# Two weight sums per seven-product block made by accumulating transfers, with two plain blocks per layer instead of three

## The chip, the cores and the metric

The kernel runs as one program on one core of a Trainium2 chip. The metric is device time in microseconds (us), from one launch with the data in the chip's memory to the output there. Engines are named as the profile does: PE multiplies matrices, DVE, ACT and POOL work on tiles in on-chip memory (POOL can't read PE's result banks, and doesn't in this kernel), and SP issues most transfers.

## The reference

Two layers of a decoder trunk over 512 tokens, with 16 learned tokens ahead of them (528 columns in layer 0; in layer 1 only the 512 real ones are carried through the projections behind attention). A layer is: RMSNorm, one input projection, an attention group and a retention group, an output projection with residual, then RMSNorm and a SwiGLU feed-forward part (FFN) with residual. All in float32. What matters here is the FFN and the output projection ahead of it:

```
h = h + einsum('blc,cd->bld', mix, w_out)          # 1024 -> 1024
hn = rmsnorm(h, ffn_norm)
ff = silu(hn @ w_gate) * (hn @ w_up)                # 1024 -> 2816, twice
h = h + ff @ w_down                                 # 2816 -> 1024
```

## The kernel before

**Precision.** Every float32 operand of a product is split into a high part (a cast to fp32r, on ACT) and a low part (the value minus its high part, on DVE or POOL). A product is three matmuls: high by high, high by low of the tokens, low of the weight by high. `convert` makes these parts for a weight tile: one cast per 128x512 half (line 180), then the subtraction (line 183), which is one 128x512 instruction on DVE, or four of 128x128 on POOL where a job has `pool` set.

**Tokens lie along columns**, 128 features to a tile, eight tiles `h[k]`. `scale_split` (lines 308, 309) makes `xh`, `xl`, the parts of the scaled tokens. The reciprocal root of the norm, `R`, is made separately (`rstd`, lines 279 to 289) from column sums of squares and multiplied in behind the products.

**The FFN** has 22 blocks of 128 gate and 128 up columns. The first `PLAIN` = 3 blocks of a layer are plain: `dense_steps` runs eight steps for the gate and eight for the up rows, three matmul pairs of 264 columns each in layer 0, three matmuls of 512 columns in layer 1. The other blocks are a `Unit`, which treats gate and up together as a 2x2 block product (rows gate and up, contraction in two halves of four tiles, `HB` = 4, tokens in two column halves of 264 or 256) and needs seven half-size products instead of eight: 84 matmuls. A unit has a head (weights `w1`, the plain gate tile), a middle (`w2`, and the first half of `w3`) and a tail (the second half of `w3`, and `w4`). `w2`, `w3` and `w4` need sums of the weight quarters (`make2`, `make3`, `make4`): four DVE instructions of 128x512 per unit, before their splits (lines 888 and 889). The tokens need sums too, made once per layer by `x_forms` during the plain blocks (four calls; lines 861 to 866, then a split into `th`, `tl`).

**Order.** The blocks go in `ROUNDS` of 3, 4, 4, 4, 4 and 3 blocks. The down-projection of a round stands between the units of the next one, one job per unit: `head, middle, down job, tail, second half of the down job`. A unit of the first round has no down job yet; it goes `head, middle`, and its tail comes behind the head of the next unit. The up product of a unit ends its tail and starts its closing chain: `done` (lines 974 to 986) adds the banks, scales, applies `silu` on ACT, multiplies by the up rows and splits the result into `ah`, `al`, which the down job of the next round multiplies. For plain blocks the same is done by `g_done` (line 836, then `silu`) and `u_done` (lines 844, 845).

PE's order is the order in which the steps are written. The other engines get theirs from the Tile scheduler, which lists each engine's instructions when the program is built; at run time each engine, and each engine's queue of transfers, takes them strictly in that order and waits at the first that isn't ready. `need` makes the weights of the coming jobs one unit ahead.

**Buffers.** Weight tiles arrive in a ring `raw` of three (512 KB each) and, for the units' up rows, `fraw` of two; the split weights sit in `whi`/`wlo` and `fwhi`/`fwlo`, two each. A load is issued by SP as soon as the last reader of the slot is done. In the plain part the reader that frees a `raw` slot is the subtraction of line 183. The first gate product of a layer is held back: its bank `psd` is read only once `R` is there (line 836, during the second gate product), so the second up product needs this bank again.

Of the kernel before, what the change touches and what calls it, by code (L numbers as in the profile page):

```python
# [20 lines left out]
DEPTH = 2  # L21
# [3 lines left out]
DFF = 2816  # L25
NF = DFF // 128
ROUNDS = ((0, 3), (3, 7), (7, 11), (11, 15), (15, 19), (19, 22))
PLAIN = 3
HB = NK // 2
EPS = 1e-6  # L30
NBLK = SEQ // 128
# [8 lines left out]
def hybrid_kernel(ctx, tc, x_t, w_in, w_fl, w_out, w_gate, w_up, w_down, vecs, b_fg, rope, decay, mask, ident, out_t):  # L40
    nc = tc.nc
# [84 lines left out]
    def vcol(c):  # L126
        return vec[:, c:c + 1]
# [58 lines left out]
    def dense_steps(src, parts, pool=False, banks=False, ahead=(1, 4), own=None, wait=None):  # L186

        j = len(jobs)  # L190
        jobs.append({"src": src, "pool": pool, "own": own})

        def chunk(k0, k, n, xs, cols, ps, done):
            def go():
                convert(j)
                if k == 0:
                    t = [psum_a() for _ in cols] if banks else psum()
                    ps.append(t)
                    ps.append(t if banks else [t[:, b] for b in range(2)])
                size = jobs[j]["w"][0][0]  # L200
                _, hi, lo = jobs[j]["w"][(k0 + k) // size]
                wk = (k0 + k) % size
                xh, xl = xs(k)
                for i, (w, x) in enumerate(((hi, xh), (hi, xl), (lo, xh))):
                    for b, (c0, c1) in enumerate(cols):
                        nc.tensor.matmul(ps[1][b][:, 0:c1 - c0], w[:, wk, :], x[:, c0:c1],  # L206
                                         start=(k == 0 and i == 0), stop=(k == n - 1 and i == 2))
# [54 lines left out]
    def fft(tag, dt=F32R, shape=(128, T), bufs=None):  # L262
        return phase["ffn"].tile(list(shape), dt, name=tag, tag=tag, bufs=bufs)
# [28 lines left out]
    RSC = -1.0 / (2.0 * D)  # L292
# [513 lines left out]
    def out_proj(l, rnd, mix, real):  # L806

        cols = REAL if real else FULL
        xs = lambda k: mix[k]["mix"]
        return sum([dense_steps(w_out[l, rnd, m2], [(4 * s, xs, 4, cols, add_h(2 * m2 + s, real)) for s in range(2)],  # L810
                                rnd == 0 or m2 < 2, rnd == 1 and m2 == 1) for m2 in range(NK // 2)], [])

    def ffn(l, st, real, last):
        QC = REAL if real else FULL
# [7 lines left out]
        def two(t):  # L822
            return t[:, t0:T].rearrange("p (a b) -> p a b", a=2)
# [30 lines left out]
        def x_forms(k):  # L854
            def go():
                if k == 0:
                    st["t"] = [[fft(f"t{p}{i}", shape=(128, 2, 4, w)) for p in "hl"] for i in range(2)]
                s = fft("S", F32, (128, 6, w), 2)
                a, b = ((h[k][:, c0:c1], h[HB + k][:, c0:c1]) for c0, c1 in HC)
                g0, g1 = vcol(V_FFN + l * NK + k), vcol(V_FFN + l * NK + HB + k)  # L860
                nc.scalar.activation(s[:, 0:2], two(h[k]), AF.Copy, scale=g0)
                nc.vector.tensor_sub(s[:, 2], s[:, 1], s[:, 0])
                for i in range(2):
                    nc.vector.scalar_tensor_tensor(s[:, 3 + i], b[1], g1, s[:, 1 + i], ALU.mult, ALU.subtract)
                nc.vector.scalar_tensor_tensor(s[:, 5], a[1], g1, s[:, 4], ALU.mult, ALU.subtract)
# [21 lines left out]
        def splits(hi, lo, src):  # L887
            nc.scalar.copy(hi, src)  # L888
            nc.vector.tensor_sub(lo, src, hi.bitcast(F32))  # L889
# [17 lines left out]
        class Unit:  # L907
# [12 lines left out]
            def load(self):  # L920
                if "a" not in self.t:
                    for n, src, pool, tag, bufs in (("a", w_gate, wp, "raw", 3), ("b", w_up, phase["ffn"], "fraw", 2)):
                        self.t[n] = pool.tile([128, NK, 128], F32, name=tag, tag=tag, bufs=bufs)
                        nc.sync.dma_start(self.t[n], src[l, self.f])


            def make1(self, hi, lo):
# [1 line left out]


            def make2(self, hi, lo):
                a, b = self.t["a"], self.t["b"]
                s = self.t["s"] = fft("S", F32, (128, NK, 128), 2)
                nc.vector.tensor_add(s[:, HB:NK], b[:, 0:HB], b[:, HB:NK])
                nc.vector.tensor_sub(s[:, 0:HB], s[:, HB:NK], a[:, 0:HB])
                splits(hi, lo, s)


            def make3(self, hi, lo):
                a, b = self.t["a"], self.t["b"]  # L940
                nc.vector.tensor_sub(b[:, 0:HB], a[:, 0:HB], b[:, 0:HB])
                splits(hi, lo, b)


            def make4(self, hi, lo):
                a, s = self.t["a"], self.t["s"]
                nc.vector.tensor_sub(a[:, HB:NK], a[:, HB:NK], s[:, 0:HB])
                splits(hi, lo, a[:, HB:NK])

            def bank(self, n):  # L950
# [21 lines left out]
            def done(self):  # L972
                e = self.t["e"]
                sg = tt("sg")
                with tc.high_priority():
                    nc.vector.tensor_add(two(sg), self.t["zy"][:, :, 0:w], e[:, 0:2])
# [72 lines left out]
        for r, (f0, f1) in enumerate(ROUNDS):  # L1049
            for f in range(f0, f1):  # L1050
                if f < PLAIN:
                    steps += dense_steps(w_gate[l, f], [(0, xs, NK, QC, g_done(f) if f else held.append)], banks=f == 1)
                    steps += dense_steps(w_up[l, f], [(0, xs, NK, QC, u_done(f))])
                    continue
                u = Unit(f)
                steps += u.head()
                for v in tails:
                    v.last()
                    steps += v.tail()
                tails = []  # L1060
                u.rest()
                steps += u.middle()
                if fills:
                    p, g0, g1 = fills.pop(0)
                    j = down_job(p, g0, g1)
                    steps += down(j, 0, 2 * p, g0, g1, not real)
                    u.last()
                    steps += u.tail()
                    steps += down(j, 1, 2 * p + 1, g0, g1, False)
                else:  # L1070
                    tails = [u]
            for p, g0, g1 in fills:
# [167 lines left out]
        return steps  # L1240

    gf = const.tile([128, NK], F32, name="gf")
    nc.vector.tensor_scalar_mul(gf, vec[:, V_FIN:V_FIN + NK], RSC)

    def layer(l):
# [177 lines left out]
```

## Time and profile before

| | before |
|---|---|
| median of 3 runs | 1268.92 us (1268.71 to 1269.12) |
| profiled execution, its own time | 1268.51 us |
| its span | 1266.7 us |
| PE busy | 1252.7 us, 99% of the span |
| DVE, ACT, POOL busy | 998.3, 686.9, 265.0 us |
| FFN, layer 0: first gate product starts; first unit starts | 287.7; 322.5 us |
| FFN, layer 1: second gate product starts; first unit starts | 923.0; 945.2 us |

The page is one execution taken by the hardware profiler. A timeline row gives the start in microseconds from the span's start, the duration, the engine, the line, the operation, the output and input tiles and shapes, how many such instructions were merged in the row, and in brackets the idle time of the engine before it with what ended it. Instructions of one engine overlap slightly: the distance between two starts is what the engine can hold, and for matmuls this distance, not the duration, is the cost.

### The profile page before, as it was taken

What the parts mean: (1) busy time and instruction counts of PE and PEld (TensorE: products, weight loads), DVE (VectorE), ACT (ScalarE), POOL (GpSimd) and SP (SyncE); (2) the same over time, 40 slices, a digit from 0 to 9 for tenths busy, and PEclk for the clock granted to TensorE, in tenths of its full rate; (3) what the DMA queues carried; (4) which work ended last, traced back from release to release, by engine and by line L of the source; (5) the groups of instructions that cost most, each with busy time, mean ns of one, the idle gap of its engine ahead of it and who ended that gap; (6) DMA issues with size and microseconds to landing.
All of it is one profiled execution on the core that took longest, in us unless ns stands there. A gap on an engine that the chain in (4) does not pass through costs nothing.

```text
span 1266.7 us, 23601 instructions
## 1 busy us (share of the span) xinstructions
PE 1252.7 (99%) x9263; PEld 1195.0 (94%) x9263; DVE 998.3 (79%) x1853; ACT 686.9 (54%) x1246; POOL 265.0 (21%) x526
## 2 busy tenths in 40 slices
PE   9999999999999999999999999999999999999997
PEld 8999999999999999999999989999789999999996
DVE  7878756879988888887786877567898878888867
ACT  7666545676444444444456665457764444444445
POOL 3455546420000000000025546454100000000000
PEclk9999999999999999999999999999999999999999
DMA  6322222223333333332323132222323333333321
GB/s 218 94 69 87 90 86 76 68 68 117 105 97 100 101 101 101 101 100 84 101 77 117 61 102 83 77 91 67 100 91 124 103 100 101 101 100 101 100 83 68
DMA packets 45680, 120.57 MB, mean 95 GB/s; under 512 B 5360, under 2 KB 12272, under 8 KB 45568
## 3 DMA queue, kind: packets, MB, share of 16 engines
q1 hardware_dynamic: 45136, 118.77, 29.5%
q8 instruction: 73, 1.20, 0.4%
q14 instruction: 39, 0.32, 0.1%
q10 hardware_dynamic: 432, 0.29, 0.1%
HBM read 116.91 MB, written 2.13 MB: 94 GB/s over the span
## 4 chain that ended last, share of the span: by engine, by line
PE 94%; DVE 2%; ACT 2%; DMA 1%; issue 0%; DVEq 0%; ACTq 0%; SPq 0%
PE psd L206 30%; PE psa L900 19%; PE psd L1035 14%; PE psd L900 13%; PE psa L206 5%; PE psa L1035 4%; PE psa L407 2%; PE psa L582 2%; PE psa L497 2%; PE psa L749 1%; PE psa L719 1%; DMA h<-x_t 0%; ACT whi L180 0%; PE psa L279 0%; ACT sq L325 0%
## 5 line engine op out<-in xcount | busy, mean ns | idle before, releaser
L183 POOL TENSOR_TENSOR wlo<-raw,whi 128x128 fp32r<-128x128 f32 x504 | 260.8, 551 | 268.1 <-ACT whi L180 247.4
L206 PE MATMUL psd<-xh,whi 128*128 128x264 f32 (+1 forms) x792 | 195.3, 314 | 0.7 <-ACT whi L180 0.6
L206 PE MATMUL psd<-xl,whi 128*128 128x264 f32 (+1 forms) x792 | 186.1, 302 | 0.6 <-DVE xl L309 0.6
L206 PE MATMUL psd<-xh,wlo 128*128 128x264 f32 (+1 forms) x792 | 186.4, 303 | 0.0
L206 PEld LDWEIGHTS psd<-xh,whi 128*128 128x128 f32 x792 | 127.9, 189 | 6.0 <-ACT whi L180 1.6
L206 PEld LDWEIGHTS psd<-xh,wlo 128*128 128x128 f32 x792 | 126.8, 188 | 6.3 <-DVE wlo L183 0.4
L206 PEld LDWEIGHTS psd<-xl,whi 128*128 128x128 f32 x792 | 127.4, 188 | 5.2 <-DVE xl L309 1.2
L180 ACT CAST whi<-raw 128x512 fp32r<-128x512 f32 (+1 forms) x168 | 98.4, 613 | 49.6 <-PE psd L206 36.5
L888 ACT CAST whi<-raw 128x1024 fp32r<-128x1024 f32 (+2 forms) x62 | 54.9, 885 | 50.9 <-PE psd L900 39.5
L888 ACT CAST fwhi<-raw 128x1024 fp32r<-128x1024 f32 (+2 forms) x62 | 55.6, 897 | 47.0 <-PE psd L900 40.0
L85 POOL MEMSET kl<- 64x528 f32 x2 | 1.1, 534 | 345.4 <-PE psa L900 345.4
L889 DVE TENSOR_TENSOR wlo<-raw,whi 128x1024 fp32r<-128x1024 f32 (+2 forms) x62 | 62.9, 1014 | 12.8 <-ACT whi L888 12.7
L889 DVE TENSOR_TENSOR fwlo<-raw,fwhi 128x1024 fp32r<-128x1024 f32 (+2 forms) x62 | 64.0, 1032 | 10.8 <-ACT fwhi L888 10.6
L900 PE MATMUL psa<-th,whi 128*128 128x264 f32 (+1 forms) x232 | 65.4, 282 | 0.0
L900 PE MATMUL psa<-th,wlo 128*128 128x264 f32 (+1 forms) x232 | 65.4, 282 | 0.0
L900 PE MATMUL psa<-tl,whi 128*128 128x264 f32 (+1 forms) x232 | 65.3, 282 | 0.0
L900 PE MATMUL psa<-th,fwhi 128*128 128x264 f32 (+1 forms) x224 | 63.4, 283 | 0.0
L900 PE MATMUL psa<-tl,fwhi 128*128 128x264 f32 (+1 forms) x224 | 63.3, 283 | 0.0
L900 PE MATMUL psa<-th,fwlo 128*128 128x264 f32 (+1 forms) x224 | 63.2, 282 | 0.0
L517 ACT ACTIVATE pd<-pd,nmax 128x144 f32<-128x144 f32 (+1 forms) x64 | 36.9, 576 | 40.7 <-DVE nmax L504 28.8
L966 ACT COPY e<-psa 128x264 f32<-128x264 f32 (+1 forms) x114 | 42.8, 375 | 28.5 <-PE psa L900 24.2
L888 ACT CAST fwhi<-S 128x1024 fp32r<-128x1024 f32 x20 | 21.0, 1049 | 68.6 <-PE psa L900 66.5
(342 smaller groups left out, 4030.3 us busy)
## 6 DMA issues: line engine op xcount, KB each, us to landing
raw<-w_in SPq DMA_DIRECT2D x54, 512.0 KB, 3.5
raw<-w_gate SPq DMA_DIRECT2D x44, 512.0 KB, 3.9
fraw<-w_up SPq DMA_DIRECT2D x38, 512.0 KB, 3.5
raw<-w_down SPq DMA_DIRECT2D x64, 256.0 KB, 2.7
raw<-w_out SPq DMA_DIRECT2D x16, 512.0 KB, 3.5
raw<-w_down SPq DMA_DIRECT2D x32, 192.0 KB, 2.5
bc<-cdr SPq DMA_DIRECT2D x16, 264.0 KB, 3.5
raw<-w_up SPq DMA_DIRECT2D x6, 512.0 KB, 3.5
```

The source lines that it names most:

```text
L180: pin(nc.scalar.copy(hi, job["raw"][:, c0:c1]), pinned)
L183: pin(sub(lo[:, i:i + wide], job["raw"][:, c0 + i:c0 + i + wide], hi[:, i:i + wide].bitcast(F32)), pinned)
L206: nc.tensor.matmul(ps[1][b][:, 0:c1 - c0], w[:, wk, :], x[:, c0:c1], start=(k == 0 and i == 0), stop=(k == n - 1 and i == 2))
L407: nc.tensor.transpose(ps[:, 128 * j:128 * j + 128], src[:, o:o + 128], idt)
L497: nc.tensor.matmul(sc[0:nq, 0:c1 - c0], st["q"][s][:, q0:q0 + nq], kk[:, c0:c1], start=(i == 0), stop=(i == 1))
L517: nc.scalar.activation(pr, pr, AF.Exp, bias=nmax[0:nq], scale=-1.0, accum_out=rsum)
L582: nc.tensor.matmul(po[:, c0:SEQ], v[:, j, :], pp[:, j, META + c0:T], start=(j == 0 and i == 0), stop=(j == 4 and i == 1))
L888: nc.scalar.copy(hi, src)
L889: nc.vector.tensor_sub(lo, src, hi.bitcast(F32))
L900: nc.tensor.matmul(bank()[:, 0:b.shape[-1]], a[:, o + k, :], b, start=(fresh and k == 0 and i == 0), stop=(k == n - 1 and i == 2), skip_gr ...
L966: nc.scalar.copy(self.t["e"][:, i], self.t["x"][:, 0:w])
L1035: nc.tensor.matmul(v[:, 0:c1 - c0], a[:, s * n + k, :], b[:, c0:c1], start=(k == 0 and i == 0), stop=(k == n - 1 and i == 2))
```

## The change

- `PLAIN` is 2: block 2 of each layer becomes a unit. It is in the first round, so it has no down job between its parts, and its tail stands behind the head of block 3.
- In a unit the sum of the up rows' two halves, and the sum of the gate's low half with the up rows' low half, are no longer made by DVE. A new tile `ws` (two buffers) receives the low half of the up rows by a plain transfer of SP, and the high half by a second transfer, issued by POOL, that adds to what is there. A third, also from POOL, adds the gate's low half onto the low half of `fraw`. `make2` keeps one DVE instruction, `make3` none. Signs differ by this (sums instead of differences), which `x_forms` and the scale in `done` take up with a negated column `ngf`.
- The low parts of the last two tiles of the output projection (`m2` = 2, 3) and of all plain gate and up tiles go to POOL, eight 128x128 instructions a tile instead of two of 128x512 on DVE.
- The scratch for the descriptors of POOL's transfers is set to 4096.

```diff
-PLAIN = 3
+PLAIN = 2
@@ out_proj
-                                rnd == 0 or m2 < 2, rnd == 1 and m2 == 1) for m2 in range(NK // 2)], [])
+                                True, rnd == 1 and m2 == 1) for m2 in range(NK // 2)], [])
@@ x_forms
+                n1 = ngf[:, l * HB + k:l * HB + k + 1]
-                nc.vector.tensor_sub(s[:, 2], s[:, 1], s[:, 0])
-                for i in range(2):
-                    nc.vector.scalar_tensor_tensor(s[:, 3 + i], b[1], g1, s[:, 1 + i], ALU.mult, ALU.subtract)
-                nc.vector.scalar_tensor_tensor(s[:, 5], a[1], g1, s[:, 4], ALU.mult, ALU.subtract)
+                nc.vector.tensor_sub(s[:, 2], s[:, 0], s[:, 1])
+                nc.vector.scalar_tensor_tensor(s[:, 3], b[1], g1, s[:, 1], ALU.mult, ALU.subtract)
+                nc.vector.scalar_tensor_tensor(s[:, 4], b[1], n1, s[:, 2], ALU.mult, ALU.subtract)
+                nc.vector.scalar_tensor_tensor(s[:, 5], a[1], n1, s[:, 4], ALU.mult, ALU.subtract)
@@ Unit.load
+                    s = self.t["s"] = fft("ws", F32, (128, NK, 128), 2)
+                    nc.sync.dma_start(s[:, HB:NK], w_up[l, self.f, :, 0:HB])
+                    nc.gpsimd.dma_start(s[:, HB:NK], w_up[l, self.f, :, HB:NK], accum_op=ALU.add)
+                    nc.gpsimd.dma_start(self.t["b"][:, 0:HB], w_gate[l, self.f, :, 0:HB], accum_op=ALU.add)
@@ make2, make3, make4
-                s = self.t["s"] = fft("S", F32, (128, NK, 128), 2)
-                nc.vector.tensor_add(s[:, HB:NK], b[:, 0:HB], b[:, HB:NK])
-                nc.vector.tensor_sub(s[:, 0:HB], s[:, HB:NK], a[:, 0:HB])
+                nc.vector.tensor_add(s[:, 0:HB], s[:, HB:NK], a[:, 0:HB])
-                nc.vector.tensor_sub(b[:, 0:HB], a[:, 0:HB], b[:, 0:HB])
-                nc.vector.tensor_sub(a[:, HB:NK], a[:, HB:NK], s[:, 0:HB])
+                nc.vector.tensor_add(a[:, HB:NK], a[:, HB:NK], s[:, 0:HB])
@@ done
-                nc.vector.scalar_tensor_tensor(u[:, c], sg[:, c], RSC, st["R"][:, c], ALU.mult, ALU.mult)
+                nc.vector.scalar_tensor_tensor(u[:, c], sg[:, c], -RSC, st["R"][:, c], ALU.mult, ALU.mult)
@@ the steps of a plain block
-                    steps += dense_steps(w_gate[l, f], [(0, xs, NK, QC, g_done(f) if f else held.append)], banks=f == 1)
-                    steps += dense_steps(w_up[l, f], [(0, xs, NK, QC, u_done(f))])
+                    steps += dense_steps(w_gate[l, f], [(0, xs, NK, QC, g_done(f) if f else held.append)], True, banks=f == 1)
+                    steps += dense_steps(w_up[l, f], [(0, xs, NK, QC, u_done(f))], True)
```

How the change moves instructions, at three places. In the lists below a row is one instruction, or several alike with their count, in the order in which the engine takes them; `raw` is a weight tile of the ring, `fraw` that of a unit's up rows, `ws` the new sum tile, `whi`/`wlo` and `fwhi`/`fwlo` the split weights.

POOL, from the output projection of layer 0 to the first units, as changed; in the kernel before there are no transfers here, and the row of x264 is one of x232 that ends with the output projection's `m2` = 1:

```order
L183 TENSOR_TENSOR wlo<-raw,whi 128x128 x264
L929 DMA fraw<-w_gate 128x512
L928 DMA ws<-w_up 128x512
L183 TENSOR_TENSOR wlo<-raw,whi 128x128 x8
L929 DMA fraw<-w_gate 128x512
L928 DMA ws<-w_up 128x512
L183 TENSOR_TENSOR wlo<-raw,whi 128x128 x8
L928 DMA ws<-w_up 128x512
L929 DMA fraw<-w_gate 128x512
```

The 32 new subtractions of the x264 are those of `m2` = 2, `m2` = 3, the first gate tile and the first up tile; the two rows of x8 are the second gate and second up tile. The accumulating transfers of blocks 2 and 3 stand ahead of them.

DVE around the making of `R` in layer 0. Before:

```order
L132 TENSOR_TENSOR tl_4309<-S,th_4308 128x1056
L288 SCALAR_TENSOR_TENSOR nwt<-psa,nwt 128x264 x2
L183 TENSOR_TENSOR wlo<-raw,whi 128x512
L289 SCALAR_TENSOR_TENSOR R<-nwt,R 128x528
L183 TENSOR_TENSOR wlo<-raw,whi 128x512
L836 SCALAR_TENSOR_TENSOR sg<-psd,R 128x528
L844 SCALAR_TENSOR_TENSOR tq<-psd,R 128x528
```

As changed:

```order
L286 TENSOR_TENSOR nwt<-R 128x528
L938 TENSOR_TENSOR ws<-ws,raw 128x512
L288 SCALAR_TENSOR_TENSOR nwt<-psa,nwt 128x264 x2
L132 TENSOR_TENSOR tl_4341<-S,th_4340 128x1056
L289 SCALAR_TENSOR_TENSOR R<-nwt,R 128x528
L890 TENSOR_TENSOR fwlo<-ws,fwhi 128x1024
L836 SCALAR_TENSOR_TENSOR sg<-psd,R 128x528
L844 SCALAR_TENSOR_TENSOR tq<-psd,R 128x528
```

The sum of block 2 (line 938), which reads `ws` behind its accumulating transfer, and the low part made from it (line 890) now stand ahead of the row that frees the bank `psd` (line 836).

ACT at the `silu` of the first gate product, layer 0, as changed:

```order
L180 CAST whi<-raw 128x512 x2
L889 CAST fwhi<-ws 128x1024
L889 CAST fwhi<-raw 128x1024
L396 ACT_TABLE_LOAD
L396 ACTIVATE sg<-sg 128x528
L889 CAST whi<-raw 128x1024
L131 CAST ah_4382<-tq 128x528
```

The casts of block 2's `w2` (from `ws`) and of block 3's gate tile (`fwhi<-raw`) stand ahead of the table load, that of block 2's own gate tile (`whi<-raw`) behind the `silu`. In the kernel before no weight cast of a unit stands in this place: the two plain casts `whi<-raw` and two token rows `S` are followed by the table load at once.

More of the change, by code (lines that the diff above doesn't have):

```diff
@@ L931, in make2 @@
             def make2(self, hi, lo):
-                a, b = self.t["a"], self.t["b"]
-                s = self.t["s"] = fft("S", F32, (128, NK, 128), 2)
-                nc.vector.tensor_add(s[:, HB:NK], b[:, 0:HB], b[:, HB:NK])
-                nc.vector.tensor_sub(s[:, 0:HB], s[:, HB:NK], a[:, 0:HB])
+                a, s = self.t["a"], self.t["s"]
+                nc.vector.tensor_add(s[:, 0:HB], s[:, HB:NK], a[:, 0:HB])
                 splits(hi, lo, s)
             def make3(self, hi, lo):
-                a, b = self.t["a"], self.t["b"]
-                nc.vector.tensor_sub(b[:, 0:HB], a[:, 0:HB], b[:, 0:HB])
-                splits(hi, lo, b)
+                splits(hi, lo, self.t["b"])
             def make4(self, hi, lo):
                 a, s = self.t["a"], self.t["s"]
-                nc.vector.tensor_sub(a[:, HB:NK], a[:, HB:NK], s[:, 0:HB])
+                nc.vector.tensor_add(a[:, HB:NK], a[:, HB:NK], s[:, 0:HB])
                 splits(hi, lo, a[:, HB:NK])
@@ L1242, in hybrid_kernel @@
     gf = const.tile([128, NK], F32, name="gf")
+    ngf = const.tile([128, DEPTH * HB], F32, name="ngf")
+    for i in range(DEPTH):
+        c = V_FFN + i * NK + HB
+        nc.vector.tensor_scalar_mul(ngf[:, i * HB:i * HB + HB], vec[:, c:c + HB], -1.0)
     nc.vector.tensor_scalar_mul(gf, vec[:, V_FIN:V_FIN + NK], RSC)
@@ L1410 @@
     }
-    nc = bacc.Bacc("TRN2", target_bir_lowering=False, num_devices=1)
+    nc = bacc.Bacc("TRN2", target_bir_lowering=False, num_devices=1, dynamic_dma_scratch_size=4096)
     arrays, args = {}, []
```

## The prediction

> **What bounds the kernel now.** I read the page first: span, busy times, the chain that ended last; then the waits of PE.
>
> ```profile
> span 1266.7 us, 23601 instructions
> PE 1252.7 (99%) x9263; PEld 1195.0 (94%) x9263; DVE 998.3 (79%) x1853; ACT 686.9 (54%) x1246; POOL 265.0 (21%) x526
> PE 94%; DVE 2%; ACT 2%; DMA 1%; issue 0%; DVEq 0%; ACTq 0%; SPq 0%
> PE psa L1276 <- DVE wide L61: 1.6, 1, 1.6
> PE psa L497 <- DVE kl L441: 0.9, 1, 0.9
> ```
>
> PE is the bound almost everywhere: 94% of the chain, and its longest single wait is 1.6 us, at the very start. So DVE work taken away is worth nothing by itself; only fewer matmuls are, and every wait that the change puts ahead of PE is lost in full. How near PE stands to waiting is seen where the first gate product hands on its bank:
>
> ```profile
> 299.34 0.40 PE L206 MATMUL psa<-xh,whi 128*128 128x264 f32 x2
> 302.58 0.70 DVE L289 SCALAR_TENSOR_TENSOR R<-nwt,R 128x528 f32<-128x528 f32 x1
> 303.20 0.68 DVE L183 TENSOR_TENSOR wlo<-raw,whi 128x512 fp32r<-128x512 f32 x1
> 303.80 0.70 DVE L836 SCALAR_TENSOR_TENSOR sg<-psd,R 128x528 f32<-128x528 f32 x1
> 305.12 0.40 PE L206 MATMUL psd<-xh,whi 128*128 128x264 f32 x2
> ```
>
> The second gate product starts at 299.34, the second up product takes the bank at 305.12, and DVE freed it at 304.5: a margin of 0.6 us.
>
> **The change: matmuls.**
>
> ```profile
> 388.28 2.92 PE psa L1035 x24
> 928.71 16.67 PE psd L206 x72
> 945.22 0.28 PE L900 MATMUL psa<-xh,whi 128*128 128x256 f32 x1
> 952.31 0.39 PE L1035 MATMUL psd<-ah,fwhi 128*128 128x512 f32 x1
> ```
>
> A matmul of 264 columns costs 2.92/24 = 0.1217 us, of 512 columns 16.67/72 = 0.2315; between 945.22 and 952.31 stand head and middle of a unit, 60 of 256 columns, 0.118 each. Layer 0: 96 become 84, 12 x 0.1217 = 1.46 us less. Layer 1: 48 x 0.2315 = 11.11 become 84 x 0.118 = 9.91, 1.20 less. Saved: 2.7 us. That is all the change can give.
>
> **POOL's low parts.** They start behind the casts of the output projection's third tile, and how long eight take depends on DVE:
>
> ```profile
> 273.87 1.14 ACT L180 CAST whi<-raw 128x512 fp32r<-128x512 f32 x2 [4.10 <-PE psd L206]
> L183 POOL TENSOR_TENSOR wlo<-raw,whi 128x128 fp32r<-128x128 f32 x504 | 260.8, 551 | 268.1 <-ACT whi L180 247.4
> 37.36 3.44 POOL L183 TENSOR_TENSOR wlo<-raw,whi 128x128 fp32r<-128x128 f32 x8 [5.22 <-ACT whi L180]
> 83.05 5.27 POOL L183 TENSOR_TENSOR wlo<-raw,whi 128x128 fp32r<-128x128 f32 x8 [4.63 <-ACT whi L180]
> 35.09 1.41 DVE L441 TENSOR_TENSOR kl<-tq,kh 64x528 fp32r<-64x528 f32 x2
> 85.31 0.96 DVE L441 TENSOR_TENSOR kl<-tq,kh 64x528 fp32r<-64x528 f32 x1
> 283.00:300.00 17.00, 17.00 (x141) 16.86 (x140) 16.93 (x30) 11.20 (x19) 0.00 (x0) 1.00 0.44 156
> ```
>
> With POOL idle the same DVE subtraction takes 0.70 us (two in 1.41), beside POOL 0.96; and eight low parts take 3.44 to 5.27. So the two slow each other. From 283 to 300 DVE is busy throughout (third figure, 16.93 of 17; POOL, the fifth, had nothing). I take 8 x 0.551 = 4.41 for the tiles of `m2` = 2 and 3, and 5.27 for the first gate and up tile: from 274.5 (first half cast), 8.8 + 10.5 us, so the first up tile's low parts end at 293.9 (292.1 with 4.41 throughout). Layer 1 begins at 898.8 and ends at 918.2:
>
> ```profile
> 898.19 1.14 ACT L180 CAST whi<-raw 128x512 fp32r<-128x512 f32 x2 [3.85 <-PE psd L206]
> ```
>
> The Trainium skill, "SBUF — State Buffer", in its table of terms, says that DVE and GpSimd share a port pair that one instruction holds in full, the other waiting. The direction agrees with 3.44 against 5.27; by its words each low part could wait out a whole DVE instruction, which is a rival below.
>
> **The accumulating transfers.** That last low part frees the `raw` slot for block 2's gate tile; SP issues it, and behind it the plain half of `ws`. POOL then waits, with the second gate tile's low parts queued behind it, until this half has landed; only then it can issue the sum.
>
> ```profile
> raw<-w_gate SPq DMA_DIRECT2D x44, 512.0 KB, 3.9
> raw<-w_down SPq DMA_DIRECT2D x64, 256.0 KB, 2.7
> ```
>
> 768 KB together: 3.9 plus the 1.2 us that 256 KB more cost between these rows, 5.1, and 0.3 for SP's second issue, 5.4 us. `ws` has its half at 299.3. An accumulating transfer is not in the trace. It reads what it adds to, so at least the 2.7 of a plain one; twice that, 5.4, and a microsecond of POOL's issue, 6.4, is my upper bound. I take 5.0, nearer the upper end, since both halves of the traffic pass the same 16 engines. The sum of layer 0 is there at 304.3.
>
> The Trainium skill, "DMA: Bandwidth & Descriptors", section "Anatomy of one DMA — SWDGE (gpsimd) path", gives 2.0 us plus bytes/436e3 for a transfer issued by GpSimd, an estimate of 2.6 us here; it doesn't say whether accumulating costs more, and no row shows it. By it the forecast would fall by about 5 us, near the cheap rival below.
>
> **Walk, layer 0.** (1) Second gate tile: first low part ready at 299.3 + 0.6 (issue) + 0.6 = 300.5; PE wants it with its third pair, 299.34 + 2 x 0.243 = 299.8. **+0.7**. (2) DVE now has the sum `ws<-ws,raw`, and behind it the two steps to `R`, a token split, `R`, the low part of `ws`, ahead of the row that frees the bank. In distances between starts (0.62 for 512 or 528 columns, 1.15 for 1024):
>
> ```profile
> 301.30 0.76 DVE L288 SCALAR_TENSOR_TENSOR nwt<-psa,nwt 128x264 f32<-128x264 f32 x2
> 300.13 1.25 DVE L132 TENSOR_TENSOR tl<-S,th 128x1056 fp32r<-128x1056 f32 x1
> 441.84 1.23 DVE L889 TENSOR_TENSOR fwlo<-S,fwhi 128x1024 fp32r<-128x1024 f32 x1 [1.80 <-ACT fwhi L888]
> ```
>
> 0.62 + 0.68 + 1.17 + 0.62 + 1.14 + 0.70 = 4.95; from 304.3 the bank is free at 309.25, and PE, 0.7 late, asks at 305.8. **+3.4** (1.1 with a transfer of 2.7; 4.8 with 6.4). (3) ACT: block 3's gate tile stands ahead of the table load and `silu`, which before ran at once:
>
> ```profile
> 302.17 1.28 ACT L396 ACT_TABLE_LOAD   x1
> 304.53 0.65 ACT L396 ACTIVATE sg<-sg 128x528 f32<-128x528 f32 x1 [1.08 <-DVE sg L836]
> ```
>
> That tile's load waits for the second gate tile's low parts, from 300 to 305.3; landed 3.9 later, 309.2, cast 1.05, load 1.28, `silu` 0.65: 312.2 instead of 305.2. What queues behind on ACT and DVE reaches the middle of block 2, with PE already 4.1 late: **+1.2** (0 to 3).
>
> (4) The first down job. A plain block 2 closes long before it is needed; a unit's tail has behind it only block 3's middle, 36 matmuls, and the two plain blocks' down steps, 12 of 264 columns: 48 x 0.1217 = 5.85 us. The closing chain of a unit:
>
> ```profile
> 442.08 0.41 PE L1035 MATMUL psd<-ah,whi 128*128 128x264 f32 x2
> 442.98 0.70 DVE L976 TENSOR_TENSOR sg<-psd,e 128x528 f32<-128x528 f32 x1
> 449.40 0.71 DVE L132 TENSOR_TENSOR al<-tq,ah 128x528 fp32r<-128x528 f32 x1
> ```
>
> The tail's product ended at 442.1, `al` was ready at 450.1, 8.0 us. **+2.0** (0 if DVE serves the chain without the work in between, 4 if it is late already).
>
> **Walk, layer 1.**
>
> ```profile
> 928.55 0.42 PE L206 MATMUL psd<-xh,whi 128*128 128x512 f32 x1
> 926.46 0.69 DVE L289 SCALAR_TENSOR_TENSOR R<-nwt,R 128x512 f32<-128x512 f32 x1
> 929.16 1.28 ACT L396 ACT_TABLE_LOAD   x1
> 930.45 0.64 ACT L396 ACTIVATE sg<-sg 128x512 f32<-128x512 f32 x1
> ```
>
> `ws` has its half at 918.2 + 5.4 = 923.6, the second gate tile's first low part is ready at 924.9; its product began 24 x 0.2315 before 928.55, at 923.0, and wants it at 923.5: **+1.4**. The sum is there at 928.6; fewer DVE rows stand behind it, some 2.2 us: 930.8 against 928.55 + 1.4, **+0.85**. Block 3's gate tile lands at 924.3 + 5.3 + 3.9 = 933.5, cast, table load and `silu` end at 936.5, and only then ACT casts block 2's gate tile and DVE makes its low part, 1.05 + 1.2: 938.7. The head of block 2 begins 24 x 0.2315 after the second up product, at 934.1 + 2.25 = 936.4, and needs the low part 0.2 later: **+2.2**. Block 3's middle, whose low part stands behind a sum of the next unit on DVE: **+1.5** (0 to 4.7, no row shows it). Down job: 36 x 0.118 and 6 x 0.2315, 5.6 against the chain's 8.0, **+2.3**.
>
> **After that** PE starts a unit every 16.0 us (84 matmuls, and 24 pairs of 0.243 of the down job); its loads go out one unit ahead:
>
> ```profile
> 447.30 0.33 SPq L924 DMA_DIRECT2D fraw<-w_up  x1
> 449.41 0.33 SPq L924 DMA_DIRECT2D raw<-w_gate  x1
> 445.00 0.28 PE L900 MATMUL psa<-xh,whi 128*128 128x264 f32 x1
> 447.90 0.28 PE L900 MATMUL psa<-th,fwhi 128*128 128x264 f32 x1
> ```
>
> The loads at 447 to 449 are for the unit whose head begins 16.0 us after 445.0, at 461.0, and whose middle, the first to multiply a sum, 2.9 later, 463.9. `ws` has its half at 449.4 + 0.3 + 3.9 = 453.6; ahead of 463.9 lie sum, cast and low part with what stands between them, some 4 us by the DVE distances above: the accumulate has until 459.9, 6.3 us. At 5.0 nothing is lost; the two DVE instructions saved per unit lie beside PE, worth nothing.
>
> **Sum.** -2.7 + (0.7 + 3.4 + 1.2 + 2.0) + (1.4 + 0.85 + 2.2 + 1.5 + 2.3) = +12.9 us on the profiled execution's 1268.5 (span 1266.7), which is 0.4 below the median: 1281.8 by the median.
>
> **Rivals.**
> - *The accumulate is cheap* (2.7 us, POOL's parts at 4.41): both sums come 2.3 to 4 us earlier; (1), (2) shrink to under 1, layer 1's bank wait goes; the down jobs and some of the ACT row stay: 0 to +6, 1269 to 1275. For it: 16 transfer engines at 44% in these 17 us.
> - *Everything hidden*, the faster side: block 2 closes in 5.6 us instead of 8.0, if DVE, with two instructions of 0.62 fewer per unit, serves each step at once. 1266.2. Against it: in the quoted chain DVE is never idle, but the work between its steps is other units' splits, which stay.
> - *POOL becomes the bound*: where it alternates with DVE it waits 0.62 per low part on top of 0.43, 8.4 us per tile; two tiles per layer 6 us later, against PE margins of about 1: +22 to +31, 1291 to 1300. Against it: the worst rows stop at 5.27.
> - *Accumulates lose the steady state*: if one takes 8 us, 1.7 over the 6.3, some 34 units lose 1.7 each: +58, 1325 and more. It decides from 6.3 us on.
>
> **Chances.** Forecast (+6 to +22) 0.62; cheap accumulate 0.16; all hidden 0.07; POOL the bound 0.07; steady state 0.08. A measurement of this kernel can tell 0.2%, 2.5 us, from no change: faster 0.07; same 0.13 (the cheap case's lower half and a part of its rest); slower 0.80. The range of the forecast alone is 1275 to 1291; down to 1268.5 it takes in the cheap case, up to 1298 most of POOL's: 1268.5 to 1298.
>
> **What would show it.** In the changed profile: waits of PE at line 206 for `wlo` from POOL in the second gate product and for the bank at the second up product; PE waiting at line 1036 for `ah`, `al` of block 2 in both layers; issues of `ws` and `fraw` on POOL's queue landing in about 5 us; units still 16.0 us apart. I am wrong if these waits are absent, if the accumulates land in under 3 us, or if every unit is longer.

## The result

The changed kernel takes 1297.12 us (median of 5, 1295.97 to 1297.34) against 1268.92 before: 1.0219 times, 95% interval 1.0209 to 1.023, 28.2 us slower. The forecast was slower by 12.9. The end of the range, 1298, just holds the time, but the sum had less than half of the loss; that end was set for POOL as the bound, a case that the runs do not show, so that it holds the time is luck.

The page of the changed kernel: span, busy times, the granted clock in 40 slices, the chain.

```profile
span 1294.2 us, 23995 instructions
PE 1259.6 (97%) x9287; PEld 1201.2 (93%) x9287; DVE 962.3 (74%) x1765; ACT 692.4 (54%) x1252; POOL 394.8 (31%) x702
PEclk9999999998999999999999999999988999999999
PE 89%; DVE 5%; DMA 3%; ACT 1%; POOL 1%; issue 1%; ACTq 0%; DVEq 0%; SPq 0%; POOLq 0%
```

The span grew by 27.5 us. PE's idle time went from 14.0 to 34.6 us, and its busy time, which should have fallen by the 2.7 us of matmuls saved, rose by 6.9: so 20.6 us are waits and 9.6 are matmuls that ran slower (the mean granted clock of the span, 0.991 against 0.998, makes some 9 of them). The clock line says where: slice 10 (291 to 324 us) and slices 30 and 31 (938 to 1003) are at 8 tenths, the entries of the two layers' FFN parts.

The waits of PE, changed kernel:

```profile
PE psa L206 <- POOL wlo L183: 8.9, 2, 6.1
PE psd L206 <- DVE sg L836: 5.7, 2, 5.2
PE psa L901 <- DVE wlo L890: 4.2, 2, 3.8
PE psa L1036 <- DVE al L132: 0.9, 1, 0.9
PE psd L1036 <- DVE al L132: 0.6, 1, 0.6
```

One line per place: second gate product for POOL's low parts (2.8 and 6.1 us in layers 0 and 1), second up product for the bank (5.2 and 0.45), the head and middle of the first units for low parts, and the first down job for block 2's `al`. They are the places that the prediction named, with other sizes. The chain view of the entry in layer 0 (start, duration, what) has both transfers of `ws` and behind them DVE, up to the row that frees the bank:

```profile
296.54 4.45 DMA ws<-w_up
301.54 4.03 DMA ws<-w_up
305.58 0.98 DVE ws L938
307.25 3.48 DVE tl L132
312.92 0.70 DVE sg L836
```

POOL's queue in the changed kernel, layer 0 and then layer 1:

```profile
274.12 21.96 POOL L183 TENSOR_TENSOR wlo<-raw,whi 128x128 fp32r<-128x128 f32 x32 [3.39 <-ACT whi L180]
301.54 0.87 POOL L928 DMA_DIRECT2D ws<-w_up  x1 [4.50 <-DVE tl L132]
302.10 3.65 POOL L183 TENSOR_TENSOR wlo<-raw,whi 128x128 fp32r<-128x128 f32 x8
...
910.39 22.01 POOL L183 TENSOR_TENSOR wlo<-raw,whi 128x128 fp32r<-128x128 f32 x32 [3.08 <-ACT whi L180]
939.34 0.86 POOL L928 DMA_DIRECT2D ws<-w_up  x1 [6.10 <-DMA ws<-w_up]
939.90 3.64 POOL L183 TENSOR_TENSOR wlo<-raw,whi 128x128 fp32r<-128x128 f32 x8
```

The four tiles took 22 us, 5.5 each, where I had 4.41 for two of them and 5.27 for two. Then POOL stands idle until the plain half of `ws` is there, 301.5 and 939.3, and the second gate tile's low parts stand behind it. These take 3.65 us, while DVE is idle for most of the time.

DVE in the same kernel, with two rows that no row of before is like:

```profile
305.58 0.98 DVE L938 TENSOR_TENSOR ws<-ws,raw 128x512 f32<-128x512 f32 x1 [3.39 <-DMA ws<-w_up]
307.17 3.56 DVE L132 TENSOR_TENSOR tl<-S,th 128x1056 fp32r<-128x1056 f32 x1
310.65 0.95 DVE L289 SCALAR_TENSOR_TENSOR R<-nwt,R 128x528 f32<-128x528 f32 x1
...
944.27 3.68 DVE L289 SCALAR_TENSOR_TENSOR R<-nwt,R 128x512 f32<-128x512 f32 x1
972.77 0.69 DVE L938 TENSOR_TENSOR ws<-ws,raw 128x512 f32<-128x512 f32 x1 [7.41 <-DMA ws<-w_up]
```

DVE waits for the accumulated sum of block 2 (3.4 us here) with the making of `R` behind it, and in layer 1 for that of block 4 (7.4 us) with the low parts behind it that PE needs in block 3. And `tl`, 1.25 us in the two rows before it, took 3.56.

The transfers, changed kernel:

```profile
fraw<-w_gate POOLq DMA_DIRECT2D x40, 256.0 KB, 4.1
ws<-w_up SPq DMA_DIRECT2D x40, 256.0 KB, 2.6
ws<-w_up POOLq DMA_DIRECT2D x40, 256.0 KB, 4.6
```

An accumulating transfer of 256 KB lands 4.1 to 4.6 us after its issue, a plain one 2.6.

### The profile page after: what moved, and what is told of

Read it like the earlier page. It is cut to its first block, busy times and chain, and to the rows that moved or that the text cites. A ratio compares the mean times of both kernels' runs of the same rounds, so it can differ in the third digit from the quotient of the medians.

```text
span 1294.2 us, 23995 instructions
## 1 busy us (share of the span) xinstructions
PE 1259.6 (97%) x9287; PEld 1201.2 (93%) x9287; DVE 962.3 (74%) x1765; ACT 692.4 (54%) x1252; POOL 394.8 (31%) x702
## 4 chain that ended last, share of the span: by engine, by line
PE 89%; DVE 5%; DMA 3%; ACT 1%; POOL 1%; issue 1%; ACTq 0%; DVEq 0%; SPq 0%; POOLq 0%
PE psd L206 26%; PE psa L901 18%; PE psd L1036 14%; PE psd L901 13%; PE psa L206 4%; PE psa L1036 4%; DMA ws<-w_up 2%; PE psa L407 2%; PE psa L582 2%; PE psa L497 2%; PE psa L749 1%; PE psa L719 1%; POOL wlo L183 1%; PE psa L368 1%; DVE fwlo L890 0%
## 5 line engine op out<-in xcount | busy, mean ns | idle before, releaser
L183 POOL TENSOR_TENSOR wlo<-raw,whi 128x128 fp32r<-128x128 f32 x600 | 323.8, 610 | 274.1 <-ACT whi L180 274.0
L206 PE MATMUL psd<-xh,whi 128*128 128x264 f32 (+1 forms) x744 | 183.7, 315 | 7.0 <-DVE sg L836 5.7
L206 PE MATMUL psd<-xl,whi 128*128 128x264 f32 (+1 forms) x744 | 174.2, 302 | 0.2 <-DVE xl L309 0.2
L206 PE MATMUL psd<-xh,wlo 128*128 128x264 f32 (+1 forms) x744 | 174.2, 303 | 0.0
L206 PEld LDWEIGHTS psd<-xh,whi 128*128 128x128 f32 x744 | 120.9, 190 | 12.1 <-issue 6.2
L928 POOL DMA_DIRECT2D ws<-w_up x40 | 35.9, 896 | 291.8 <-DVE h L1043 247.8
L206 PEld LDWEIGHTS psd<-xh,wlo 128*128 128x128 f32 x744 | 119.7, 189 | 5.1
L206 PEld LDWEIGHTS psd<-xl,whi 128*128 128x128 f32 x744 | 120.4, 190 | 3.8 <-DVE xl L309 0.6
L929 POOL DMA_DIRECT2D fraw<-w_gate x40 | 35.4, 884 | 210.5 <-DMA fraw<-w_up 149.6
L889 ACT CAST fwhi<-ws 128x1024 fp32r<-128x1024 f32 x22 | 23.1, 1048 | 74.8 <-PE psa L901 66.2
```

The lines of the kernel that those rows point to most:

```text
L183: pin(sub(lo[:, i:i + wide], job["raw"][:, c0 + i:c0 + i + wide], hi[:, i:i + wide].bitcast(F32)), pinned)
L928: nc.gpsimd.dma_start(s[:, HB:NK], w_up[l, self.f, :, HB:NK], accum_op=ALU.add)
L929: nc.gpsimd.dma_start(self.t["b"][:, 0:HB], w_gate[l, self.f, :, 0:HB], accum_op=ALU.add)
```

## Experiments: the parts of the change, alone and in pairs

The change has three parts that can be switched apart: two plain blocks (`PLAIN`), low parts on POOL, accumulating sums. Six kernels give, with before and after, all eight combinations; their edits are the same lines of the change, put in or left out.

**Two plain blocks alone.**

> The kernel before with two plain blocks instead of three, nothing else of the change. Theory (the loss is made by the accumulating transfers waiting behind low parts that are late on POOL): only the matmuls saved, -2.7 us, the closing chain of block 2 ahead of the first down job, 1.0 us per layer as the changed kernel's trace has it, and some lateness of the token forms: 0 to +6 us, 1269 to 1275. Rival (a unit in place of the third plain block is itself too tight for DVE and ACT): +14 us or more, with waits of PE in block 2.

```diff
-PLAIN = 3
+PLAIN = 2
```

Measured 1288.96 us, ratio 1.0160 (1.0143 to 1.0177): 20.1 slower. The rival holds.

**The accumulating sums alone**, with three plain blocks and low parts on DVE:

> The kernel before with the two accumulating sums alone: three plain blocks, low parts on DVE. Theory: the sums have a whole plain block more time and nothing stands ahead of them on POOL: 0 to +2 us, units 16.0 us apart. Rival (accumulating transfers crowd the transfer engines or hold DVE up wherever they are): +8 to +15 us, spread over the units too.

Measured 1269.62, 1.0006 (0.9997 to 1.0016): nothing.

**POOL's low parts alone**:

> The kernel before with the low parts of the last projection tiles and of all plain tiles on POOL, three plain blocks, sums on DVE. Theory: eight low parts take 5.5 us beside a busy DVE, four tiles in a row end 22 us after the first cast, but no transfer waits behind them: 0 to +5 us, with PE waiting for low parts or the bank for no more than 3 us at a time. Rival (POOL is the bound by itself): +10 us or more, PE waiting for POOL's low parts in both layers.

```diff
-                                rnd == 0 or m2 < 2, rnd == 1 and m2 == 1) for m2 in range(NK // 2)], [])
+                                True, rnd == 1 and m2 == 1) for m2 in range(NK // 2)], [])
-                    steps += dense_steps(w_gate[l, f], [(0, xs, NK, QC, g_done(f) if f else held.append)], banks=f == 1)
+                    steps += dense_steps(w_gate[l, f], [(0, xs, NK, QC, g_done(f) if f else held.append)], True, banks=f == 1)
-                    steps += dense_steps(w_up[l, f], [(0, xs, NK, QC, u_done(f))])
+                    steps += dense_steps(w_up[l, f], [(0, xs, NK, QC, u_done(f))], True)
```

Measured 1283.72, 1.0119 (1.0104 to 1.0134): 14.9 slower, the rival's size, but not in its way: PE waits for the bank and for casts, not for POOL's low parts. Its waits:

```profile
PE psd L206 <- DVE sg L836: 5.1, 2, 2.8
PE psd L206 <- ACT whi L180: 3.7, 3, 2.6
```

**The change without accumulates** (two plain blocks, POOL's low parts):

> The change without its accumulating transfers: two plain blocks, low parts on POOL, the four sums per unit on DVE. Theory: without the sums behind the late low parts the long waits (3.0 and 5.4 us in layer 0, 6.3 and 3.9 in layer 1) and the lowered clock behind them are gone; what stays is the closing chain and late token forms: +2 to +8 us, 1271 to 1277. Rival (two plain blocks with POOL's low parts are enough for the loss): +18 us or more.

Measured 1286.16, 1.0133 (1.0118 to 1.0149): 17.3 slower, the rival's side.

**The change without POOL's low parts**:

> The change without POOL's low parts: two plain blocks, accumulating sums, low parts of the plain tiles on DVE. Theory now (DVE's preparation for the units, above all the token forms, fills the plain blocks and is the bound there; two plain blocks are 16 steps too short for it): the sums by transfer take some 1.2 us per unit off DVE, the rest is as with two plain blocks alone (1289): 1282 to 1290. Rival (accumulating transfers make the loss beyond two plain blocks): 1294 or more.

Measured 1292.80, 1.0188 (1.0173 to 1.0203): 24.0 slower, between the two.

**The change with three plain blocks**:

> The change with three plain blocks: accumulating sums and POOL's low parts. Theory: POOL's low parts alone cost 15 us with three plain blocks; with the accumulates behind them on POOL's queue the sums come late as well, so more than the 15.6 us of the two apart: 1287 to 1295. Rival (the parts simply add): 1284 to 1286.

Measured 1290.69, 1.0168 (1.0153 to 1.0183): 21.9 slower, more than the two parts added, 15.6.

| us over before (1268.9) | three plain blocks | two plain blocks |
|---|---|---|
| neither | 0 | 20.1 |
| accumulating sums | 0.8 | 24.0 |
| POOL's low parts | 14.9 | 17.3 |
| both | 21.9 | 28.2 |

So my theory, that the loss comes from accumulates standing behind late low parts, falls as the main cause: without any accumulate 17 of the 28 us are there. Two plain blocks alone cost 20, POOL alone 15, and the two together 17, so they look like two ways of meeting one limit. The accumulates cost nothing alone and 4 to 11 us on top of one of these or both.

## Experiments: what the limit is

What is special about the plain blocks is seen in one row of before: the stretch from the second gate product to the first unit (columns as in the prediction's windows row: PE, its weight loads, DVE, ACT, POOL, clock).

```profile
299.30:322.40 23.10, 23.10 (x194) 23.10 (x193) 23.10 (x39) 14.32 (x20) 0.00 (x0) 1.00 0.21 64
```

PE and DVE are both busy for all of 23.1 us. DVE makes the token forms and `R` there. With two plain blocks PE's cover shrinks by 96 matmuls, 11.7 us in layer 0, and DVE has block 2's sums and low parts to make besides. The chain view of two plain blocks alone, layer 0, stays on DVE from 292.28 until PE starts at 321.70, but for 3.1 us without a named cause; its first and last rows there, and PE's:

```profile
292.28 1.81 DVE wlo L183 x3
320.39 1.26 DVE tl L132
321.70 0.81 PE psa L900 x2
```

**Less DVE work.** Two plain blocks, and the low parts of the token forms left out:

> Two plain blocks alone, with the low parts of the token forms left out: four DVE instructions of 128x1056 fewer per layer, 4.7 us, the high part multiplied in their place, so PE's work is the same. Theory (DVE is the bound of the entry to the units): PE's waits in block 2 shrink by about these 4.7 us per layer, and the lowered clock with them: 1275 to 1281. Rival (ACT's casts, or the loads, set when the forms are ready): 1287 or more.

```diff
-                split(th, tl, s[:, 2:6])
+                nc.scalar.copy(th, s[:, 2:6])
-            return lambda k: [t[:, k % 2, i] for t in st["t"][k // 2]]
+            return lambda k: [st["t"][k // 2][0][:, k % 2, i]] * 2
```

Measured 1278.42, 1.0074 (1.0057 to 1.0091): 10.5 us less than two plain blocks alone, for 9.4 us of DVE instructions taken away (four of 1.17 us per layer). DVE's preparation sets the time of the entry. The other 9.7 us over before stay: PE still waits 5.8 us for the casts of the token forms, which start when DVE has made the forms. Whether another order of DVE's rows would save time with the same work was not tried.

**More cover.** Four plain blocks:

> The kernel before with four plain blocks instead of three. Theory (three plain blocks already cover DVE's preparation, two are too short): only the matmuls are paid, 1.46 + 1.20 = 2.7 us, with no new wait over 1 us: 1270 to 1274. Rival (each plain block is worth much in cover, 20 us from two to three, and some is left to gain): faster than 1268.

```diff
-PLAIN = 3
+PLAIN = 4
```

Measured 1272.44, 1.0026 (1.0016 to 1.0036): 3.5 us (2.0 to 4.6) slower, the matmuls and no more. Three blocks are just enough cover; the third was not spare.

**POOL beside DVE.** In place of the subtractions of the last projection tiles and the plain tiles POOL writes zeros, 3.8 us a tile:

> Three plain blocks, sums on DVE, and for the last two projection tiles and the plain tiles POOL writes zeros (eight writes of 128x512 per tile, some 4.2 us, as long as eight low parts) instead of subtracting: low parts of these tiles are left out, POOL is as busy, but reads nothing. Theory (POOL's subtraction and DVE's instructions slow each other where both read on-chip memory): DVE runs at its usual speed and PE does not wait for the bank: 1268 to 1273. Rival (POOL's place in the order, its lateness, makes the 15 us of the low parts on POOL): 1280 or more.

```diff
+            if job["pool"] and "plain" in job:
+                for _ in range(4):
+                    nc.gpsimd.memset(lo.bitcast(F32), 0.0)
+                job["split"] = c1
+                continue
             wide = 1 if job["pool"] else c1 - c0
```

(Only the jobs of these tiles carry the mark `plain`; the lines that set it are left out here.)

Measured 1271.12, 1.0017 (1.0008 to 1.0027): 2.2 us slower, against 14.9 with the subtractions. The busy times of the engines and one DVE instruction in POOL's kernel, then the same in this one with POOL's writes (columns of an instruction: count, busy time, mean ns, idle time before):

```profile
PE 1259.4 (98%) x9263; PEld 1199.3 (94%) x9263; DVE 997.8 (78%) x1821; ACT 687.4 (54%) x1246; POOL 354.8 (28%) x654
L329 DVE TENSOR_TENSOR ss<-ss,sq 128x512 f32<-128x512 f32 x7 | 6.1, 871 | 0.1
```

```profile
PE 1252.9 (99%) x9263; PEld 1196.1 (94%) x9263; DVE 981.9 (77%) x1821; ACT 687.7 (54%) x1246; POOL 325.2 (26%) x654
L336 DVE TENSOR_TENSOR ss<-ss,sq 128x512 f32<-128x512 f32 x7 | 4.8, 684 | 0.1
L183 POOL MEMSET wlo<- 128x512 f32 x128 | 60.7, 526 | 27.7 <-PE psd L213 24.0 <-PE psa L213 3.7
```

Beside POOL's subtractions DVE's additions of two on-chip tiles take 871 ns, beside its writes 684, as with POOL idle. Both kernels take the same subtractions off DVE, and 1821 instructions stay with it. With POOL's writes DVE is busy for 16.4 us less than before (998.3), and with POOL's subtractions 15.9 of them are back. The two kernels differ in what POOL reads, and also in that the writes let go of the weight tile earlier. That has a share in the 12.6 us between them: in POOL's kernel a wait of PE of 2.6 us in layer 0 goes back to a load that was issued at 321.4, as soon as POOL's last low part of that tile ended. How large the share is in all stays open; the durations above do not depend on it.

The Trainium skill, "SBUF — State Buffer", section "SBUF: two separate sides", names as rivals for the port pair of DVE and GpSimd a DVE instruction with two inputs in on-chip memory and a GpSimd instruction that reads there: the 684 ns beside pure writes agree. That the loser waits out whole instructions is not the price here: eight low parts took 5.5 us beside a busy DVE, where the alternation priced in the prediction would take 8.4.

## Experiments: the lowered clock

Behind a wait in two plain blocks alone the matmuls stood farther apart. PE's timeline there:

```profile
320.31 0.59 PE L900 MATMUL psa<-th,fwhi 128*128 128x264 f32 x1 [4.43 <-ACT th L131]
321.70 0.59 PE L900 MATMUL psa<-tl,fwhi 128*128 128x264 f32 x1 [0.80 <-DVE tl L132]
322.09 0.42 PE L900 MATMUL psa<-th,fwlo 128*128 128x264 f32 x1
322.31 0.42 PE L900 MATMUL psd<-th,fwhi 128*128 128x264 f32 x1
```

After 4.4 us of waiting a matmul of 264 columns starts every 0.22 us instead of 0.12. To separate the clock from late operands, matmuls that nothing needs were put into the wait:

> Two plain blocks alone, and 18 matmuls of 512 columns (4.2 us) that nothing needs, put where PE waits 4.4 us for the token forms in block 2 of each layer. Theory (a wait of some us lowers the clock granted to PE behind it, 2 to 2.5 us per place): the fillers cost nothing inside the wait and the matmuls behind it run at their usual spacing: 3 to 5 us less than two plain blocks alone, 1284 to 1286. Rival (the slow matmuls behind the wait have another cause, operands that come late): 1289 or more.

```diff
+                def busy():
+                    idle = psum_a()
+                    for _ in range(18):
+                        nc.tensor.matmul(idle, ones, st["x"][0][0][:, 16:528], start=True, stop=True)
+                if self.f == PLAIN:
+                    first.insert(2, busy)
```

Measured 1284.67, 1.0123 (1.0108 to 1.0138): 4.3 us less than without them, with 8.3 us more work for PE (36 x 0.2315). The windows of the wait and behind it, of two plain blocks alone and then with the fillers (clock in the third figure from the end):

```profile
314.00:320.20 6.20, 1.12 (x8) 0.91 (x7) 6.17 (x10) 2.88 (x4) 0.00 (x0) 0.78 0.28 85
320.20:324.00 3.80, 2.89 (x11) 2.59 (x12) 3.80 (x7) 0.96 (x3) 0.00 (x0) 0.50 0.19 24
324.00:328.00 4.00, 4.00 (x22) 4.00 (x21) 1.88 (x3) 1.22 (x2) 0.00 (x0) 0.54 0.28 113
```

```profile
314.00:320.20 6.20, 5.45 (x28) 4.32 (x27) 6.20 (x10) 2.88 (x5) 0.00 (x0) 1.00 0.28 80
320.20:324.00 3.80, 2.57 (x17) 2.07 (x16) 3.77 (x6) 1.96 (x3) 0.00 (x0) 1.00 0.03 12
324.00:328.00 4.00, 4.00 (x35) 4.00 (x34) 3.94 (x7) 1.81 (x3) 0.00 (x0) 1.00 0.46 131
```

The clock was granted at 0.50 for some 7 us behind the wait, and at 1.00 with PE kept busy through it. The Trainium skill, "TensorE: Matmul & The Clock Gate", section "Part 1: The HAM clock gate (the "warmup" mystery)", says that PE falls to half its clock after an idle window of about 3.4 us; the 0.50 agrees. The prediction had no such term. In the changed kernel 20.6 us of waits come with 9.6 us of slower matmuls: a wait of PE is paid about one and a half times there, once as idle time, and again as slow matmuls. It shows at three places:

```profile
299.50:322.00 22.50, 14.46 (x100) 14.06 (x98) 18.27 (x25) 11.64 (x17) 11.75 (x19) 0.85 0.54 133
930.00:960.00 30.00, 22.98 (x102) 18.35 (x101) 24.31 (x31) 16.49 (x22) 13.16 (x24) 0.89 0.52 133
968.00:984.00 16.00, 11.70 (x67) 10.16 (x66) 9.81 (x15) 4.04 (x8) 2.62 (x3) 0.79 0.73 163
```

0.15 x 22.5, 0.11 x 30 and 0.21 x 16 make some 10 us of clock not granted, a part of it while PE waited anyway.

Windows of 1 us show when the clock changes. In the changed kernel:

```profile
311.00:312.00 1.00, 0.00 (x0) 0.00 (x0) 1.00 (x2) 1.00 (x1) 1.00 (x3) 0.95 0.92 166
318.00:319.00 1.00, 1.00 (x8) 1.00 (x7) 1.00 (x3) 0.00 (x0) 0.00 (x0) 0.63 0.00 0
```

By the means 0.95 and 0.63 the clock fell to half at 311.9 and was back at 318.7, 6.8 us later. Read in the same way it fell at 940.0 and 974.1 as well, each time for 6.8 us; in two plain blocks alone for 10.2 us in layer 0 and 6.8 in layer 1, in the change without accumulates three times for 3.4. All are one, two or three times 3.41 us, and 940.0 and 974.1 lie ten times 3.41 us apart. So the clock of these traces changes on a grid of 3.41 us that does not start with the wait: it fell 3.4, 5.3 and 2.3 us into the three waits of the changed kernel (5.2, 6.1 and 3.8 us long), and a wait of 2.8 us left it at 1.00 there (until 302.9), while in the kernel with POOL's low parts alone 3.4 us at half came behind one of 2.8 us (until 309.8).

## Experiments: where the accumulates cost

The change, with the first two units' sums made by DVE again:

> The change with the sums of the first two units of each layer (blocks 2 and 3) made by DVE, those of all later units by accumulating transfers. Theory (the accumulates cost time only at the entry, where they queue behind POOL's late low parts and hold the next low parts and DVE): the time of the change without accumulates, 1286: 1284 to 1289, and no wait of PE for POOL's low parts. Rival (the accumulates cost some tenths of a microsecond in every unit): 1293 to 1297.

```diff
+                    if self.f >= PLAIN + 2:
                         nc.sync.dma_start(s[:, HB:NK], w_up[l, self.f, :, 0:HB])
                         nc.gpsimd.dma_start(s[:, HB:NK], w_up[l, self.f, :, HB:NK], accum_op=ALU.add)
                         nc.gpsimd.dma_start(self.t["b"][:, 0:HB], w_gate[l, self.f, :, 0:HB], accum_op=ALU.add)
@@ make2
+                if self.f < PLAIN + 2:
+                    nc.vector.tensor_add(s[:, HB:NK], b[:, 0:HB], b[:, HB:NK])
@@ make3
+                if self.f < PLAIN + 2:
+                    nc.vector.tensor_add(b[:, 0:HB], a[:, 0:HB], b[:, 0:HB])
```

Measured 1292.9, 1.0188 (1.0171 to 1.0205): neither. PE no longer waits for POOL's low parts, as the theory had it, but 24.0 us are lost, not 17. DVE of this kernel shows one place:

```profile
333.69 0.69 DVE L942 TENSOR_TENSOR ws<-ws,raw 128x512 f32<-128x512 f32 x1 [6.16 <-DMA ws<-w_up]
```

The first accumulated sum is now block 4's, and DVE, which takes its rows in order, stands 6.2 us for it, with the closing chain of block 2 behind. So the entry may be longer than two units. With the first five excepted (`PLAIN + 5` in the three conditions):

> The change with the sums of the first five units of each layer (blocks 2 to 6, the entry and one round more) made by DVE, those of the 15 later units by accumulating transfers. Theory (in the entry DVE reaches a sum before its transfer has landed, and stands in order behind it; with the first two units excepted the third one met the same, 6.2 us of idle DVE; past the entry the sums are early enough): as the change without accumulates, 1286: 1284 to 1288, with no wait of PE above 1 us outside the entry. Rival (wherever the first accumulating unit follows units that sum on DVE, its transfers come late and cost some 5 us): 1291 or more, with the wait of DVE for the sum tile moved to block 6 or 7.

Measured 1286.69, 1.0142 (1.0125 to 1.0159), as without accumulates (1286.16). Its waits above 1 us in the FFN parts all stand in the entries (they end at 310.6, 940.1 and 954.7 us):

```profile
PE psd L206 <- DVE sg L836: 4.5, 1, 4.5
PE psd L206 <- ACT fwhi L889: 4.0, 1, 4.0
PE psa L901 <- DVE tl L132: 1.4, 1, 1.4
```

So past the entry the accumulates are free, and within it they cost 11 us of the 28: the changed kernel against the change without them.

## Why the prediction was wrong

- **The matmuls saved**, -2.7: borne out by the other direction, four plain blocks, +3.5 (2.0 to 4.6).
- **Two steps failed.** The sum had 15.6 us of waits and nothing for slower matmuls; measured are 20.6 and 9.6. So of the 14.6 us that it lacks (27.5 less 12.9) 9.6 are a term that was put at nothing, and 5.0 are waits that came out longer than their terms.
- **"Every wait that the change puts ahead of PE is lost in full"** priced a wait once. Behind the long ones the clock was at half: 9.6 us of slower matmuls. Before has no wait above 1.6 us, so its trace could not show it.
- **"DVE work taken away is worth nothing by itself; only fewer matmuls are"** was read from the whole span, where it is true, and not from the stage of the change. I quoted DVE's 16.93 of 17 us just ahead of this stage, and used it to price POOL alone. Where two engines are both full, taking 11.7 us from the one leaves the other as the bound: I should have set the 23.1 us of DVE work, less the third plain block's own rows, against PE's new 11.4, with block 2's sums on top. I had +1.2 in layer 0, +2.2 and +1.5 in layer 1 for what DVE and ACT are late in the units; two plain blocks alone lose 20.1, and with POOL's low parts, but no accumulates, 17.3. In the changed kernel DVE itself stands idle for late sums, so there the loss lies on the path from POOL's late low parts over the transfers to DVE.
- **POOL's low parts.** The slowing was read rightly from 0.70 against 0.96 and 3.44 against 5.27, but charged to POOL's side alone. DVE's additions of two on-chip tiles ran some 27% slower (871 against 684 ns) while POOL's four tiles took their 22 us. POOL's side too was too short: four tiles ended at 296.1, not 293.9, and these 2.2 us make (1) 0.7 + 2.2 = 2.9, as measured (2.8). In layer 1 the tiles took 2.6 us more than predicted and the plain half of `ws` 1.5 more (939.3 is 6.9 behind the low parts' end, for 5.4), which is 5.5 of the 6.1 that 1.4 became.
- **(2) the bank**, +3.4: measured 5.2. The row `tl` of 3.56 instead of 1.25, 2.3 us, is more than the difference; the accumulate itself was over-estimated (the sum began 4.0 us after POOL's issue, for 5.0). In layer 1 0.45 for 0.85, since PE was later already.
- **(3), (4).** `silu`'s lateness did not reach PE in layer 0. The down jobs waited 0.9 and 0.6 us by the waits view, for 2.0 and 2.3. The head of block 2 in layer 1 waited 0.5 us for 2.2. Block 3 in layer 1: 3.8 us for 1.5, within the bounds I gave (0 to 4.7).
- **The rivals.** The cheap and the all-hidden case had the DVE bound against them as well. The case of POOL as the bound gave the time (1291 to 1300), by a mechanism that the runs do not show: low parts took 5.5 us a tile, not 8.4. The steady state held, as predicted: with the accumulates of the later units alone the time is that without any, 1286.69 against 1286.16.

The terms as measured: -2.7, waits 20.6, slower matmuls 9.6 make the 27.5 us of the span.

## What to carry to other kernels

Ask of a stage, not of the span, which engines are full in it: where a second engine is as full as the one that ends last, work that looks dear on the first is the cover of the second, and removing it loses time. Price a helper engine that reads the same memory by what it does to the engine it helps; here POOL took 15 us of subtractions off DVE in the two layers (24 of 0.62) and slowed what was left. And let a wait on PE as long as those here, 4 to 6 us, count one and a half times, or fill it.

## What was not expected of the hardware

- PE's granted clock falls to half in a wait of 4 to 6 us and stays there for one, two or three times 3.41 us, 3.4 to 10.2 us; the waits of 0.9 and 2.8 us in the changed kernel left it at 1.00, but behind one of 2.8 us in another it fell.
- DVE slows beside POOL where POOL reads (871 against 684 ns), not where POOL writes only.
- Twice, where POOL issued two accumulating transfers in a row and eight low parts behind them, a DVE instruction took 3.56 and 3.68 us instead of 1.25 and 0.69. Without POOL's low parts no DVE instruction was stretched so; nor was one in the change with three plain blocks, though POOL has the same sequence there (308.7 to 309.9 us). What held it stays open.
